# Hybrid decoder layer in float32: the first dilated group projected by token classes, its values re-sorted through DRAM

## Chip, cores and metric

One core of one Trainium2 chip runs the whole kernel. The metric is the device time of one execution in microseconds, as the median of several runs; lower is better.

## What is computed

Two layers, each on 512 tokens of width 1024, all in float32. A layer normalises `x`, multiplies it with one wide matrix `w_in`, and feeds three token mixers: a short gated convolution, a multi-head latent attention (MLA, 8 heads) and a dilated attention with 3 groups of 8 heads. The change touches the dilated attention alone:

```python
DIL_PATTERNS = ((128, 1), (512, 4), (2048, 16))       # (window, dilation) of the groups 0, 1, 2
dq = rmsnorm(dq.reshape(B, S, DIL_GROUPS, DIL_HEADS, DIL_HEAD_DIM), dil_q_norm_g[:, None, :])
dk = rmsnorm(dk.reshape(B, S, DIL_GROUPS, DIL_HEADS, DIL_HEAD_DIM), dil_k_norm_g[:, None, :])
dv = dv.reshape(B, S, DIL_GROUPS, DIL_HEADS, DIL_HEAD_DIM)
for gi, (window, dilation) in enumerate(DIL_PATTERNS):
    o_g, lse_g = dilated_group_attention(dq[:, :, gi], dk[:, :, gi], dv[:, :, gi], slopes[gi],
                                         dilation, window // dilation)
alpha = jax.nn.softmax(jnp.stack(lses, axis=0), axis=0)
o_c = jnp.sum(alpha[..., None] * jnp.stack(outs, axis=0), axis=0)
```

Group 0 attends to neighbouring tokens, so it works on four chunks of 128 consecutive tokens. Groups 1 and 2 attend to tokens 4 and 16 apart, so they work on four classes of 128 tokens, the tokens of one residue modulo 4.

## The kernel before

Products. TensorE multiplies float32 as three products of exact halves, `hi*hi + hi*lo + lo*hi`. `mm3` (L124) issues them, one line each: L126, L127 and L128. Weights are loaded into `wraw` by SyncE (L112), copied to the high half `whi` by ScalarE (L120) and reduced to the low half `wlo` by GpSimd or VectorE (L121); `wraw` has 5 buffers, and so have `whi` and `wlo`. The normalised input lies in `hhi` and `hlo`, 128 features by 512 tokens for each of 8 feature blocks.

Order of the tokens. The 512 columns of `hhi` and `hlo` are sorted by residue modulo 4: the columns of class r are 128 columns in a row (`of_class`, L175), and the tokens of a natural chunk c are every fourth column (`of_chunk`, L171).

The dilated projection. For each pair of heads p (0 to 3) and each group g (0 to 2), `dil_group` (L557) loads four weight tiles and runs `proj_n` (L147). This takes four token blocks, and in each 8 feature blocks by 3 products, so 96 matmuls for one p and g. The tokens are the stationary operand (128 columns of `hhi` or `hlo`, loaded anew for each matmul), and 384 columns of weights (q, k and v of two heads) move. Group 0 takes its tokens with `of_chunk`, groups 1 and 2 with `of_class`:

```python
yield from proj_n(wq, 384, of_class if g else of_chunk, evac)
```

After a token block, `evac` (L575) has ScalarE copy q and k to `nat` (L576) and the values to `vt` (L577). When the four blocks are done, VectorE and ScalarE find the norms (L584 to L587, L101 to L106), and GpSimd scales `nat` (L591). `dil_t` (L594) then transposes q and k: four TensorE transposes fill the four 128-column parts of one PSUM tile (L601), and ScalarE and VectorE copy the tile out (L611 to L620).

The attention of a pair. `dil_main` (L773) runs the scores (L646, L650, L656), their maxima and exponentials (L664, L667), a joint softmax over the groups whose sums go through DRAM twice (`dil_weights`, L672, with SyncE's L677, L679, L702 and L703), the scaling (L714, L718), more transposes (L734, L743) and the product with the values (`dil_pv`, L749, with the matmul on L765).

The order of the work. TensorE's order is written out by hand: `filler` (L887) is a list of projection steps, three matmuls in each, and the attention of MLA and of the dilated pairs is put between them at fixed numbers of steps. `dil_t` of a group stands 20 steps into the next projection (`T_LAG`). The other queues are ordered by a scheduler, and weight loads have a priority that lets them run ahead (L109). SyncE issues all DMAs in one queue, and one that waits holds up all behind it.

Of the kernel before, what the change touches and what calls it, by code (L numbers as in the profile page):

```python
# [28 lines left out]
C8, C2, W_RAW, W_BUF = 2, 38, 5, 5  # L29
# steps of projection between the steps of attention  # L30
F_LORA, F_P1, F_P2, F_MLA, F_TAIL, N_TAIL = 24, 6, 10, 1.2, 5.0, 28
# [9 lines left out]

# columns of the packed per-layer parameters
O_NORM, O_BG, O_CW, O_CB = 0, 8, 32, 44
# [4 lines left out]
def hybrid_kernel(ctx: ExitStack, tc: tile.TileContext, a: dict):  # L48
# [29 lines left out]

    # ---- constants
    ident = cp.tile([P, P], F32, name="ident")  # L80
# [14 lines left out]

    # ---- helpers
    def rsqrt(y, v, shape):
        """y = v ** -0.5 by Newton steps from the exponent-halving start."""
        sh = sp.tile(shape, I32, tag="rs_i", name=nm("rs_i"), bufs=3)
        t = sp.tile(shape, F32, tag="rs_t", name=nm("rs_t"), bufs=3)  # L100
        nc.vector.tensor_scalar(out=sh, in0=v.bitcast(I32), scalar1=1, scalar2=None, op0=ALU.logical_shift_right)  # L101
        nc.vector.tensor_scalar(out=y.bitcast(I32), in0=sh, scalar1=-1, scalar2=0x5F3759DF, op0=ALU.mult, op1=ALU.add)
        for _ in range(3):
            nc.vector.scalar_tensor_tensor(out=t, in0=y, scalar=-0.5, in1=v, op0=ALU.mult, op1=ALU.mult)
            nc.vector.tensor_tensor(out=t, in0=t, in1=y, op=ALU.mult)
            nc.vector.scalar_tensor_tensor(out=y, in0=t, scalar=1.5, in1=y, op0=ALU.add, op1=ALU.mult)  # L106
# [17 lines left out]
    def mm3(out, lhs, rhs, start, stop):  # L124
        """float32 product from exact halves: hi.hi + hi.lo + lo.hi"""
        nc.tensor.matmul(out, lhs[0], rhs[0], start=start, stop=False)  # L126
        nc.tensor.matmul(out, lhs[0], rhs[1], start=False, stop=False)  # L127
        nc.tensor.matmul(out, lhs[1], rhs[0], start=False, stop=stop)  # L128
# [6 lines left out]
    def proj_t(wsrc, box, X=None):  # L135
        """[128 features, 512 tokens] of h @ w for one 128-column tile of w_in; the PSUM tile goes to box;
        with X the unscaled input takes the place of h"""
        hi, lo = split_weights(1024, [(0, 1024, lambda t: t.rearrange("p (k n) -> p k n", k=KD), wsrc)])
        ps = psum("pj")
        for k in range(KD):  # L140
            cs = slice(k * P, (k + 1) * P)
            rhs = (X["hi"][k], X["lo"][k]) if X else (hhi[:, k], hlo[:, k])
            mm3(ps, (hi[:, cs], lo[:, cs]), rhs, k == 0, k == KD - 1)
            yield
        box.append(ps)

    def proj_n(wq, width, tok, evac):  # L147
        """[128 tokens, width] of h @ w per token block; wq: 4 split tiles of two k-chunks"""
        for c in range(NCH):
            ps = psum("pj")  # L150
            for k in range(KD):
                hi, lo = wq[k // 2]
                cs = slice((k % 2) * width, (k % 2 + 1) * width)
                mm3(ps[:, :width], (tok(hhi[:, k], c), tok(hlo[:, k], c)), (hi[:, cs], lo[:, cs]), k == 0, k == KD - 1)
                if k == KD - 1:
                    evac(c, ps)
                yield
# [10 lines left out]
    def tok_nat(c):  # L168
        return slice(c * P, (c + 1) * P)

    def of_chunk(t, c):  # L171
        """columns of the tokens of natural chunk c"""
        return t[:, c::NCH]

    def of_class(t, r):  # L175
        """columns of the tokens of residue r modulo 4"""
        return t[:, r * P:(r + 1) * P]
# [17 lines left out]
    def new_x(first=False):  # L195
        """x, x * gain in split form, and the running sum of squares"""
        return {"x": [], "hi": [], "lo": [], "acc": small([P, S], "acc", 1), "first": first}
# [15 lines left out]

    # products of a constant wake the tensor engine's clock while the first loads run
    wake = t2([P, P])
# [8 lines left out]
    for l in range(DEPTH):  # L224
        w_in = a["w_in"][l].rearrange("(k p) n -> p k n", p=P)
        last = l == DEPTH - 1

        # ---- low-rank inputs of the MLA branch from x * gain; the row scales follow
        lat = t8([P, NCH, W_LORA])
# [20 lines left out]
        def row_scale():  # L250
            """rows' rsqrt(mean(x ** 2) + eps)"""
            psv = psum("tr")
            for c in range(NCH):
                nc.tensor.matmul(psv[:, c:c + 1], of_chunk(X["acc"], c), ones, start=True, stop=True)
            v = small([P, NCH], "nv")
            r = small([P, NCH], "nr")
            nc.vector.tensor_scalar(out=v, in0=psv[:, :NCH], scalar1=1.0 / D, scalar2=EPS, op0=ALU.mult, op1=ALU.add)
            rsqrt(r, v, [P, NCH])
            return r
# [20 lines left out]

        # ---- h = rmsnorm(x), split
        psr = psum("tr")
# [13 lines left out]

        # derived parameters
        prm2 = small([P, 24 + 4], "prm2")
# [24 lines left out]
        def rope(dst, src, which, shape):  # L323
            """dst = rope(src * gain); shape [P, NCH, (heads,) 32]"""
            ta = rt[:, which, 0]
# [30 lines left out]
        def gate_y(y, which, f, zs):  # L356
            """y * silu(z), once both are there"""
            if (which, f) not in half_y:
                half_y[which, f] = zs
                return  # L360
            zs = half_y[which, f] if zs is None else zs
            nc.vector.scalar_tensor_tensor(out=y[f], in0=y[f], scalar=0.5, in1=zs, op0=ALU.mult, op1=ALU.mult)  # L362

        # ---- MLA
        ob = {}
# [4 lines left out]
        def mla_prep_w(p):  # L370
            """an even pair of heads brings the query weights of the next pair along"""
            o = 0 if p % 2 else 768
# [149 lines left out]
        def mla_main():  # L522
            """yields after each step on the tensor engine"""
            prep = iter(())
# [26 lines left out]

        # ---- dilated attention
        oc = {}
# [3 lines left out]
        def dil_group(p, g):  # L557
# [20 lines left out]

            yield from proj_n(wq, 384, of_class if g else of_chunk, evac)
            s2 = small([P, 16], "s16a")  # L580
# [13 lines left out]
        def dil_t(p, g):  # L594
# [3 lines left out]
            for i in range(2):  # L598
                ps = psum("tr")
                for c in range(NCH):  # L600
                    nc.tensor.transpose(ps[:, tok_nat(c)], nat[:, c, i * P:(i + 1) * P], ident)  # L601
                gg = prm2[:, 24 + g:25 + g] if i == 0 else prm[:, O_DK + g:O_DK + g + 1]
                if g == 0:
                    # per head: queries as high over low, keys as high over high, and the low keys of both heads
                    st = [t2([P, S], F32R) for _ in range(2)]
# [66 lines left out]
        def dil_weights(p):  # L672
            """maxima and sums of the strided groups to the natural order, joint weights, and back"""
            m = dil[p]
# [45 lines left out]
        def dil_trans(p, h):  # L720
            """transposed weights: g0 by key chunk, then g1, g2"""
            m = dil[p]
# [3 lines left out]
            for j2 in range(2):  # L726
# [10 lines left out]
                yield  # L737
            # the weights of g2 are zero outside the diagonal blocks of 32
            p2 = t2([P, S])
# [9 lines left out]
        def dil_pv(p):  # L749
            """the two heads fill the two halves of the array's columns"""  # L750
            m = dil[p]
# [21 lines left out]
        def dil_main(p):  # L773
            """yields the number of filler steps that follow"""
            for _ in dil_scores(p):
# [11 lines left out]
        def silu2(ps):  # L787
            """2 * silu(z) = z * (tanh(z / 2) + 1)"""
            th = t2([P, S])
            nc.scalar.activation(th, ps, AF.Tanh, scale=0.5)  # L790
            nc.vector.scalar_tensor_tensor(out=th, in0=th, scalar=1.0, in1=ps, op0=ALU.add, op1=ALU.mult)  # L791
            return th
# [9 lines left out]
        def conv_tile(f):  # L802
# [21 lines left out]
            for d in (1, 2):  # L824
                # the tokens d before, by the runs that the order of the columns leaves
                runs = [(cv[:, d * P:S], ac[:, 0:S - d * P])]
# [9 lines left out]

        # ---- gates, branch outputs, merge
        ys = {}
# [46 lines left out]

        # ---- schedule of the branches: projections fill the tensor engine while attention waits for other engines
        def filler():  # L887
# [53 lines left out]

        # ---- output projection and residual
        w_o = a["w_o"][l].rearrange("(k p) n -> p k n", p=P)
# [26 lines left out]
def _reorder(t):  # L970
    """tokens (first axis) by their residues modulo 4 and 16, the four chunks interleaved"""
    return t.reshape(4, 8, 4, 4, -1).transpose(3, 2, 1, 0, 4).reshape(t.shape)
# [6 lines left out]
def _constants():  # L979
# [6 lines left out]

    # tokens 128 h + 16 l + 4 j + r, in the order of (r, j, l, h)
    tok = _reorder(np.arange(S))
# [64 lines left out]
```

## Time and profile before

| what | value |
|---|---|
| median of 3 runs | 1546.23 us (1545.94 to 1547.9) |
| span of the profiled execution | 1547.1 us |
| TensorE matmuls busy | 1504.4 us, 97% |
| TensorE weight loads busy | 1327.6 us, 86% |
| VectorE, ScalarE, GpSimd busy | 799.7, 701.9 and 561.5 us |
| DMA | 132.14 MB, 85 GB/s over the span |

The profiled execution is known by its span alone; no time outside of it is listed. The span lies inside the range of the runs, 0.9 us above their median. PE is TensorE's row of matmuls, PEld its row of weight loads, which overlaps with PE; DVE is VectorE, ACT ScalarE, POOL GpSimd, and SPq the queue of SyncE. "L126" is line 126 of the kernel. The length of a matmul in the trace counts its way through the array as well, so the distance between the starts of two neighbours says what one costs.

### The profile page before, as it was taken

What the parts mean: (1) busy time and instruction counts of PE and PEld (TensorE: products, weight loads), DVE (VectorE), ACT (ScalarE), POOL (GpSimd) and SP (SyncE); (2) the same over time, 40 slices, a digit from 0 to 9 for tenths busy, and PEclk for the clock granted to TensorE, in tenths of its full rate; (3) what the DMA queues carried; (4) which work ended last, traced back from release to release, by engine and by line L of the source; (5) the groups of instructions that cost most, each with busy time, mean ns of one, the idle gap of its engine ahead of it and who ended that gap; (6) DMA issues with size and microseconds to landing.
All of it is one profiled execution on the core that took longest, in us unless ns stands there. A gap on an engine that the chain in (4) does not pass through costs nothing. (4 is left out here: it accounts for less than half of the span.)

```text
span 1547.1 us, 21464 instructions
## 1 busy us (share of the span) xinstructions
PE 1504.4 (97%) x7838; PEld 1327.6 (86%) x7838; DVE 799.7 (52%) x2120; ACT 701.9 (45%) x1600; POOL 561.5 (36%) x348
## 2 busy tenths in 40 slices
PE   8889999999999999999999899999999999999998
PEld 8777899999897878888898689999999888788887
DVE  7757675455555552221666767746463657411221
ACT  5445566637373533222344365646364545322220
POOL 5444243132224434444243433323122254344441
PEclk9999999999999999999999999999999999999999
DMA  8222113233243333333532311223132333233322
GB/s 234 58 82 55 42 51 82 56 83 80 59 111 89 83 82 95 96 104 103 179 97 72 86 35 42 54 70 98 47 92 62 98 97 96 82 95 96 109 82 82
DMA packets 230331, 132.14 MB, mean 85 GB/s; under 512 B 17745, under 2 KB 222929, under 8 KB 230225
## 3 DMA queue, kind: packets, MB, share of 16 engines
q1 hardware_dynamic: 230224, 130.77, 31.0%
q8 instruction: 62, 1.02, 0.3%
q14 instruction: 45, 0.36, 0.1%
HBM read 126.35 MB, written 4.39 MB: 85 GB/s over the span
## 5 line engine op out<-in xcount | busy, mean ns | idle before, releaser
L121 POOL TENSOR_TENSOR wlo<-wraw,whi 128x1024 fp32r<-128x1024 f32 (+1 forms) x184 | 426.3, 2319 | 665.5 <-ACT whi L120 643.5
L120 ACT CAST whi<-wraw 128x1024 fp32r<-128x1024 f32 (+4 forms) x249 | 235.6, 950 | 374.9 <-issue 191.4
L126 PE MATMUL pj<-hhi,whi 128*128 128x512 f32 x760 | 307.5, 405 | 0.6 <-DVE c L791 0.6
L127 PE MATMUL pj<-hlo,whi 128*128 128x512 f32 x760 | 298.7, 393 | 0.4 <-POOL hlo L290 0.4
L128 PE MATMUL pj<-hhi,wlo 128*128 128x512 f32 x760 | 299.0, 393 | 0.0
L126 PE MATMUL pj<-whi,hhi 128*128 128x384 f32 x768 | 293.7, 382 | 0.0
L127 PE MATMUL pj<-wlo,hhi 128*128 128x384 f32 x768 | 274.5, 357 | 0.0
L128 PE MATMUL pj<-whi,hlo 128*128 128x384 f32 x768 | 274.5, 357 | 0.0
L126 PEld LDWEIGHTS pj<-whi,hhi 128*128 128x128 f32 x768 | 179.8, 234 | 5.8 <-issue 2.1
L127 PEld LDWEIGHTS pj<-wlo,hhi 128*128 128x128 f32 x768 | 182.0, 237 | 0.8 <-DVE wlo L121 0.2
L128 PEld LDWEIGHTS pj<-whi,hlo 128*128 128x128 f32 x768 | 181.4, 236 | 0.0
L128 PEld LDWEIGHTS pj<-hhi,wlo 128*128 128x128 f32 x760 | 143.8, 189 | 31.2
L126 PEld LDWEIGHTS pj<-hhi,whi 128*128 128x128 f32 x760 | 144.4, 190 | 28.9 <-DVE c L791 1.4
L127 PEld LDWEIGHTS pj<-hlo,whi 128*128 128x128 f32 x760 | 144.3, 190 | 25.2 <-POOL hlo L290 0.8
L872 DVE SCALAR_TENSOR_TENSOR c<-c,sc 128x512 f32<-128x512 f32 x48 | 32.7, 685 | 239.8 <-PE sc L128 239.8
L121 DVE TENSOR_TENSOR wlo<-wraw,whi 128x768 fp32r<-128x768 f32 (+3 forms) x65 | 77.0, 1185 | 50.5 <-ACT whi L120 27.2
L667 ACT ACTIVATE c<-c,e 128x128 f32<-128x128 f32 (+1 forms) x192 | 79.9, 418 | 49.2 <-DVE e L664 49.2
L480 POOL TENSOR_SCALAR c<-c,mst 128x128 f32<-128x128 f32 (+1 forms) x64 | 35.7, 558 | 143.4 <-DVE mst L479 115.7
L591 POOL TENSOR_TENSOR c<-c,s16c 128x512 f32<-128x512 f32 x48 | 49.1, 1045 | 94.4 <-DVE s16c L106 94.4
L585 DVE TENSOR_REDUCE s16a<-c 128x8 f32<-128x512 f32 x48 | 32.7, 681 | 85.3 <-ACT c L584 85.1
L126 PE MATMUL sc<-c,whi 128*128 128x512 f32 x192 | 75.4, 393 | 0.0
L664 DVE CUSTOM_DVE_ANT_0 c<-sc,bias 128x128 f32<-128x128 f32 (+1 forms) x192 | 52.4, 319 | 44.2 <-PE sc L650 30.4
(201 smaller groups left out, 2435.5 us busy)
## 6 DMA issues: line engine op xcount, KB each, us to landing
wraw<-w_in SPq DMA_DIRECT2D x96, 512.0 KB, 3.9
wraw<-w_in SPq DMA_DIRECT2D x192, 192.0 KB, 2.8
wraw<-w_o SPq DMA_DIRECT2D x16, 512.0 KB, 4.3
bias<-bias SPq DMA_DIRECT2D x8, 512.0 KB, 3.6
wraw<-w_out_a SPq DMA_DIRECT2D x8, 512.0 KB, 3.4
wraw<-w_out_b SPq DMA_DIRECT2D x8, 512.0 KB, 3.4
wraw<-w_out_c SPq DMA_DIRECT2D x8, 512.0 KB, 3.4
wraw<-w_in SPq DMA_DIRECT2D x7, 416.0 KB, 3.5
```

The lines of the kernel that those rows point to most:

```text
L120: nc.scalar.copy(hi[:, c], raw[:, c])
L121: eng.tensor_sub(lo[:, c], raw[:, c], hi[:, c])
L126: nc.tensor.matmul(out, lhs[0], rhs[0], start=start, stop=False)
L127: nc.tensor.matmul(out, lhs[0], rhs[1], start=False, stop=False)
L128: nc.tensor.matmul(out, lhs[1], rhs[0], start=False, stop=stop)
L480: nc.gpsimd.tensor_scalar(out=pr[:, :n_], in0=pr[:, :n_], scalar1=st[:, 3:4], scalar2=1.0, op0=ALU.mult, op1=ALU.mult)
L585: nc.vector.reduce_sum(s2[:, 4 * c:4 * c + 8], sq[:, c:c + 2].rearrange("p c (h d) -> p (c h) d", d=64), axis=AX.X)
L591: eng.tensor_tensor(out=nv[:, i:i + 8], in0=nv[:, i:i + 8], in1=r2[:, i:i + 8].unsqueeze(2).to_broadcast([P, 8, 64]), op=ALU.mult)
L664: nc.vector.tensor_tensor_reduce(dst, src, b, op0=ALU.add, op1=ALU.min, scale=1.0, scalar=HIGHEST, accum_out=mc)
L667: nc.scalar.activation(dst, dst, AF.Exp, bias=mc, scale=-1.0, accum_out=sc_)
L872: nc.vector.scalar_tensor_tensor(out=ths[e], in0=ths[e], scalar=1.0, in1=ps, op0=ALU.add, op1=ALU.mult)
```

## The change

Group 0 projects classes of tokens as the other groups do, so its stationary operand is 128 columns in a row. What comes out is in the order of the classes, and two things bring it back to the order of the chunks. For q and k, each transpose writes to the PSUM tile with steps: the 128 columns of class c go to columns 32c to 32c + 31 of all four chunks. For the values, `vt` is written to a scratch in DRAM in one order and read back in the other.

```diff
-    def proj_n(wq, width, tok, evac):
+    def proj_n(wq, width, evac):
...
-                mm3(ps[:, :width], (tok(hhi[:, k], c), tok(hlo[:, k], c)), (hi[:, cs], lo[:, cs]), k == 0, k == KD - 1)
+                mm3(ps[:, :width], (of_class(hhi[:, k], c), of_class(hlo[:, k], c)), (hi[:, cs], lo[:, cs]), k == 0, k == KD - 1)
...
-            yield from proj_n(wq, 384, of_class if g else of_chunk, evac)
+            yield from proj_n(wq, 384, evac)
+            if g == 0:
+                vscr = dp.tile([S, P], F32, tag="vscr", name=nm("vscr"))
+                nc.sync.dma_start(vscr.rearrange("(r p) d -> p r d", p=P), vt)
+                nc.sync.dma_start(vt, vscr.rearrange("(p c) d -> p c d", p=P))
...
-                    nc.tensor.transpose(ps[:, tok_nat(c)], nat[:, c, i * P:(i + 1) * P], ident)
+                    dst = ps.rearrange("p (c x) -> p x c", c=NCH)[:, 32 * c:32 * c + 32] if g == 0 else ps[:, tok_nat(c)]
+                    nc.tensor.transpose(dst, nat[:, c, i * P:(i + 1) * P], ident)
```

The orders of TensorE, VectorE, ScalarE and GpSimd stay as they are, instruction by instruction; only SyncE's queue has new rows, 16 of them. In the new kernel all line numbers behind the change are 5 to 7 higher.

TensorE, the transposes of q and k of pair 1, group 0, in layer 0, before (`tr` is the PSUM tile, the third name is `nat`):

```order
L126 MATMUL pj_3140<-whi_3010,hhi 128x384
L127 MATMUL pj_3140<-wlo_3011,hhi 128x384
L128 MATMUL pj_3140<-whi_3010,hlo 128x384
L601 MATMUL tr_3153<-ident,c_599_2769 128x128 x4
L601 MATMUL tr_3164<-ident,c_599_2769 128x128 x4
L126 MATMUL pj_3140<-whi_3017,hhi 128x384
```

and the same place with the change:

```order
L126 MATMUL pj_3146<-whi_3016,hhi 128x384
L127 MATMUL pj_3146<-wlo_3017,hhi 128x384
L128 MATMUL pj_3146<-whi_3016,hlo 128x384
L608 MATMUL tr_3159<-ident,c_600_2772 128x32x4 x4
L608 MATMUL tr_3170<-ident,c_600_2772 128x32x4 x4
L126 MATMUL pj_3146<-whi_3023,hhi 128x384
```

Nothing moved there; the eight transposes write 32 runs of 4 scattered columns where they wrote 128 in a row.

SyncE's queue at the end of pair 1, group 0, before (`wraw` are weight loads, `bias` is the mask of the next pair, `scr` and `en` the first trip of the softmax sums through DRAM):

```order
L112 DMA wraw_3493<-w_in 128x3x128 x2
L112 DMA wraw_3500<-w_in 128x3x128 x2
L560 DMA bias_2739<-bias 128x2x512
L677 DMA scr_3178<-e_619_2901 128x4x8
L679 DMA en_3180<-scr_3178 128x32
L112 DMA wraw_3507<-w_in 128x3x128 x2
```

and with the change:

```order
L112 DMA wraw_3499<-w_in 128x3x128 x2
L112 DMA wraw_3506<-w_in 128x3x128 x2
L583 DMA vscr_2980<-c_601_2773 128x4x128
L584 DMA c_601_2773<-vscr_2980 128x512
L560 DMA bias_2742<-bias 128x2x512
L684 DMA scr_3184<-e_620_2904 128x4x8
L686 DMA en_3186<-scr_3184 128x32
L112 DMA wraw_3513<-w_in 128x3x128 x2
```

The two DMAs of the values stand ahead of the mask, of the softmax sums and of the next weights. It is the same for pairs 2 and 3.

SyncE's queue at the end of pair 0, group 0, before:

```order
L112 DMA wraw_2524<-w_in 128x3x128 x2
L112 DMA wraw_2741<-w_in 128x3x128 x2
L112 DMA wraw_2748<-w_in 128x3x128 x2
L112 DMA wraw_2755<-w_in 128x3x128 x2
L112 DMA wraw_2762<-w_in 128x3x128 x2
```

and with the change:

```order
L112 DMA wraw_2527<-w_in 128x3x128 x2
L112 DMA wraw_2744<-w_in 128x3x128 x2
L583 DMA vscr_2100<-c_368_1718 128x4x128
L584 DMA c_368_1718<-vscr_2100 128x512
L112 DMA wraw_2751<-w_in 128x3x128 x2
L112 DMA wraw_2758<-w_in 128x3x128 x2
```

Here only weight loads stand behind them, from the second tile of pair 1, group 0 on.

## Rows read from the trace of the kernel before

**Rows 1.** Part 1 of the page: busy us of each engine, share, instructions.

```profile
PE 1504.4 (97%) x7838; PEld 1327.6 (86%) x7838; DVE 799.7 (52%) x2120; ACT 701.9 (45%) x1600; POOL 561.5 (36%) x348
```

**Rows 2.** Waits of PE: who <- for whom, us in total, times, longest.

```profile
PE tr L455 <- DVE c L428: 10.5, 4, 4.1
PE tr L601 <- POOL c L591: 10.1, 11, 1.9
PE tr L491 <- DVE s24d L106: 3.8, 2, 1.9
```

**Rows 3.** Timeline of PE, pair 1, group 0: start us, us, instruction.

```profile
278.55 0.54 PE L126 MATMUL pj<-whi,hhi 128*128 128x384 f32 x1
278.93 0.41 PE L127 MATMUL pj<-wlo,hhi 128*128 128x384 f32 x1
...
281.48 0.39 PE L127 MATMUL pj<-wlo,hhi 128*128 128x384 f32 x1
...
285.92 0.39 PE L128 MATMUL pj<-whi,hlo 128*128 128x384 f32 x1
```

**Rows 4.** Timeline of PE, pair 1, group 1.

```profile
302.43 1.03 PE L601 MATMUL tr<-ident,c 128*128 128x128 f32 x8
303.22 0.42 PE L126 MATMUL pj<-whi,hhi 128*128 128x384 f32 x1
303.48 0.34 PE L127 MATMUL pj<-wlo,hhi 128*128 128x384 f32 x1
...
305.91 0.33 PE L126 MATMUL pj<-whi,hhi 128*128 128x384 f32 x1
```

**Rows 5.** Weight loads by line, 282 to 286 us (group 0): busy, mean ns.

```profile
L126 PEld LDWEIGHTS pj<-whi,hhi 128*128 128x128 f32 x7 | 2.3, 330 | 0.0
```

**Rows 6.** The same, 295.5 to 299 us (group 1).

```profile
L128 PEld LDWEIGHTS pj<-whi,hlo 128*128 128x128 f32 x5 | 0.9, 188 | 0.0
```

**Rows 7.** Timeline of PE, the MLA inputs, tokens by chunk, 416 columns.

```profile
11.00 0.40 PE L126 MATMUL pv<-whi,c 128*128 128x416 f32 x1
11.24 0.40 PE L127 MATMUL pv<-wlo,c 128*128 128x416 f32 x1
```

**Rows 8.** Timeline of PE, values: group 0 (PSUM in steps), then group 1.

```profile
337.99 1.73 PE L765 MATMUL pv<-c,c 128*64 128x256 f32 x16
...
341.32 1.09 PE L765 MATMUL pv<-c,c 128*64 128x128 f32 x16
```

**Rows 9.** Part 6 of the query on DMAs: KB each, median us to landing.

```profile
xr<-xnext SPq DMA_DIRECT2D x8, 256.0 KB, 2.8
xnext<-c SPq DMA_DIRECT2D x8, 256.0 KB, 2.0
```

**Rows 10.** Timeline of ACT, last copy of pair 1, group 0.

```profile
292.59 0.26 ACT L577 COPY c<-pj 128x128 f32<-128x128 f32 x1
```

**Rows 11.** Timeline of SPq, around the mask of the next pair.

```profile
301.10 0.37 SPq L560 DMA_DIRECT2D bias<-bias  x1
```

**Rows 12.** Timeline of SPq, a load behind pair 0, group 0.

```profile
218.39 0.90 SPq L112 DMA_DIRECT2D wraw<-w_in  x2
```

**Rows 13.** Timeline of ACT, the cast of those weights.

```profile
257.23 0.83 ACT L120 CAST whi<-wraw 128x768 fp32r<-128x768 f32 x1 [0.50 <-PE pj L128]
```

**Rows 14.** Timeline of POOL, scaling of pair 0, group 1.

```profile
249.05 2.05 POOL L591 TENSOR_TENSOR c<-c,s16c 128x512 f32<-128x512 f32 x2 [2.19 <-DVE s16c L106]
```

**Rows 15.** Timeline of PE, the transposes of pair 0, group 1.

```profile
252.34 1.03 PE L601 MATMUL tr<-ident,c 128*128 128x128 f32 x8
```

**Rows 16.** Windows: stretch and length, busy us (instructions), granted clock, DMA share, GB/s.

```profile
178.00:213.00 35.00, 35.00 (x188) 34.64 (x188) 23.81 (x71) 21.01 (x57) 11.21 (x14) 1.00 0.14 36
213.00:226.00 13.00, 13.00 (x88) 12.45 (x88) 10.64 (x33) 8.03 (x22) 6.00 (x7) 1.00 0.34 89
1231.90:1234.30 2.40, 2.40 (x10) 2.30 (x9) 2.37 (x11) 0.74 (x2) 0.00 (x0) 0.51 0.00 0
```

## The prediction

> **What bounds the kernel now.** I read the busy times first: TensorE's matmuls are busy 97% of the span, VectorE 52% and the others less, apart from TensorE's own weight loads at 86% [rows 1]. The list of its waits comes next: the longest entries are 10.5, 10.1 and 3.8 us [rows 2], small beside 1547. So time is what TensorE needs for its own list of instructions, and an edit counts by what it does to the pace of that list, or by a new wait on it.
>
> The pace is read from the timeline, from the start of one matmul to the start of the next. In group 0 of pair 1, 19 matmuls of 384 columns start between 281.48 and 285.92, one each 234 ns [rows 3]. In group 1 of the same pair, with the same shape, 14 start between 303.48 and 305.91, one each 174 ns [rows 4]. The reader should see that the difference is not in the moving columns. It is in the weight loads: one takes 330 ns where the tokens lie every fourth column [rows 5], and 188 ns where they lie in a row [rows 6]. A third place has stepped tokens too, the inputs of MLA: 416 columns move there, more than 384, and the distance is 0.24 us again [rows 7]. With stepped tokens the load sets the pace, whatever moves.
>
> **The change, part by part.**
>
> *The projection of group 0.* There are 4 pairs in 2 layers, and 96 matmuls in each, so 768. In TensorE's written order 104 of them come right behind an instruction of something else (27 in pair 0 of a layer, 7 in pair 1, 9 in pairs 2 and 3), and 664 behind another of the same projection. The 664 go from 234 to 174 ns each [rows 3, 4]: 664 x 0.060 = 39.8 us. The first one behind another instruction is slower in both groups: 278.55 to 278.93 is 0.38 us in group 0, 303.22 to 303.48 is 0.26 us in group 1 [rows 3, 4]. So 104 x 0.12 = 12.5 us. Together 52.3 us, all on the engine that sets the end.
>
> *The transposes of q and k.* 64 of them (8 in each group 0) now write to PSUM in steps of 128 elements. Eight of them take the 0.79 us from 302.43 to 303.22, 0.10 us each [rows 4]. No row has this step. The nearest one has steps of 4 elements: the product with the values writes so in group 0 (L761). Its 16 matmuls in the trace are, by the code, 12 of 256 columns and 4 of 128, and take 1.73 us. Group 1 writes in a row, and 16 of 128 columns take 1.09 us [rows 8]. Two heads run side by side, so these are 6 x 2 + 2 = 14 units of 128 columns against 8. The difference of 0.64 us for 6 units is 0.107 us a unit, and 8 units at that price and a tail of 0.2 us are the 1.09. A write with steps of 4 costs nothing there. I take nothing. The other end is that each new transpose takes twice its time, 64 x 0.10 = 6.4 us; below nothing is excluded, as the same columns pass.
>
> The Trainium skill (PSUM — Partial Sum Buffer, Specifications) says that PSUM has lines of 8 bytes and that any access pattern that is not contiguous slows matmuls significantly. That speaks against these writes, and by it the gain would be smaller by 6.4 us or more. The rows with steps of 4 elements, 16 bytes, do not agree with it, but no row has steps of 512 bytes.
>
> *The values through DRAM.* 8 writes and 8 reads of 256 KB. The rows have both kinds: 2.0 us to landing for a write of this size, 2.8 us for a read [rows 9]. With two issues of 0.4 us the trip takes some 5.5 us. In bytes it is 4.2 MB more on 132 MB, and the DMA engines are busy for 14 to 34% in these stretches [rows 16]. The price lies in SyncE's queue, which stands still during the trip. In pair 1 the last values are copied out at 292.85 [rows 10], so the trip ends at about 298.4. Next behind it is the mask, which goes out at 301.10 today, since it waits for the scores [rows 11]. 2.7 us remain. In pairs 2 and 3 the order is the same. In pair 0 weight loads stand behind: the first goes out at 218.39 [rows 12] and might go out 1 or 2 us later; its weights are not cast before 257.23, as the buffer behind it is not free [rows 13]. Nothing waits. The values themselves are used a whole pair later. I take nothing; the other end is under rival D.
>
> *What a faster group 0 brings forward.* Behind the end of each group 0 the work stands as now, since the orders of the four engines don't change. Inside it, a step of three matmuls shrinks from 0.70 to 0.52 us, and other engines have less time between steps. Pair 0 has the least room, with MLA beside it. VectorE is busy for 23.81 of 35 us there, and would be for 23.81 of some 28, 85%; in the 13 us behind it, it is at 10.64, 82%, while TensorE is busy throughout [rows 16]. So that load is borne today. The narrowest spot that I found is the transposes of pair 0, group 1: GpSimd is done at 251.10 [rows 14], TensorE needs it at 252.34 [rows 15], 1.2 us later. If VectorE comes out of the shorter stretch with a backlog of 2 us, about 1 us is lost here. I put 1 us for both layers, with bounds of 0 and the price of rival B.
>
> **The sum.** 52.3 - 0 - 0 - 1 = 51 us off the profiled execution's 1547.1, so 1496. The runs' median lies 0.9 us below that execution, so I forecast **1495.5 us** for the median. The gain is 3.3%.
>
> **The rivals.**
>
> *A. The forecast*, 1491 to 1503.
>
> *B. The other engines become late.* The faster group 0 takes away the room of VectorE, ScalarE and GpSimd, and TensorE waits for the preparation of MLA heads or for scaled q and k. For: such waits are there already [rows 2], and what waits is ordered by hand in steps, which get shorter. After TensorE had waited for its transposes near 1230 us the granted clock was 0.51 for 2.4 us, its lower level of 1.2 GHz [rows 16], which lost about half of these 2.4 us. Against: the 82% stretch runs without a wait, and pairs 1 to 3 have little beside group 0. Price: one more set like the existing entries of MLA (10.5 + 3.8 us for both layers [rows 2]), with 4 slow stretches at 1.2 us, is 19 us; half a set is 8. So 1503 to 1515.
>
> *C. The stepped writes to PSUM are slow*: 6.4 us at twice the time, 19 us at four times. So 1502 to 1515. For: the step is 32 times that of the nearest row. Against: that row shows no cost at all. The rule of the Trainium skill's page on PSUM, cited above, would give this rival.
>
> *D. SyncE's queue becomes the bound, and the kernel slower than before.* The two DMAs stand ahead of the mask and of the softmax sums of the pair before. A trip longer than 5.5 + 2.7 = 8.2 us holds the sums up, then the joint weights on VectorE, then the scaling of q and k of the next group behind them in that queue, and the transposes that TensorE has 20 steps into it wait for this today already (10.1 us in all [rows 2]). It decides in pairs 1 to 3, so 6 times. To end slower it has to lose 51 / 6 = 8.5 us each, a trip of over 17 us; at 20 us the time is 1496 + 6 x 11.8 = 1567. For: a queue in order, and a read that waits for the landing of the write. Against: the rows of such transfers, 2.0 and 2.8 us.
>
> *E. The pace of group 0 has another cause than the step of its tokens*, and the change brings nothing: 1546 to 1549. Against: the weight loads of MLA's inputs.
>
> **How the numbers follow.** A 0.72, B 0.13, C 0.08, D 0.02, E 0.03, and 0.02 for what I don't see. The range of 8 in 10 begins at 1490, a little under A's end for a term that I rounded down, and goes to 1510, which takes in A and about half of B and C. 0.2%, 3 us, is about what a measurement of this kernel can tell from no change. Faster by more than that are A, B, C: 0.94 with part of the unseen. No change 0.02, slower 0.04, D and parts of E and the unseen.
>
> **What would show it.** The weight loads of group 0 at 188 ns instead of 330, and its matmuls 174 ns apart. The eight groups shorter by 6 to 8 us each. The new transposes 0.10 us apart, or, for C, 0.2 and more. The write and the read of the values landing within 6 us of the last copy, and the mask's DMA still waiting for the scores; for D, the mask and the sums issued as soon as the read has gone out, and longer waits on the transposes in group 2. For B, new entries in the list of TensorE's waits in pair 0, and a granted clock under 1 behind them. The forecast is wrong if the time is over 1503: then the list of waits tells B from D, and the transposes tell C.

## The result, and the profile of the changed kernel

The changed kernel takes 1497.9 us (median of 4 runs, 1494.7 to 1499.6); the kernel before, run beside it, takes 1546.6 us. The ratio is 0.968, 95% interval [0.967, 0.970]: faster by 3.2%. On two later occasions the same kernel took 1501.9 and 1500.2 us, both 0.970 of the kernel before beside it. 1495.5 us was forecast, with a range of 1490 to 1510.

The changed lines moved the code down: what was L601 is L608 (the transposes of q and k), L591 is L596 (GpSimd's scaling). The values are written at L583 and read back at L584.

Busy time first, part 1 of the page of the changed kernel, against [rows 1]:

```profile
span 1495.3 us, 21490 instructions
PE 1451.1 (97%) x7838; PEld 1272.1 (85%) x7838; DVE 797.4 (53%) x2120; ACT 699.3 (47%) x1600; POOL 559.5 (37%) x348
```

TensorE has the same 7838 matmuls and is still busy for 97%. It is faster by being faster at its own list, not by waiting less. The timeline of TensorE in pair 1, group 0 of the changed kernel (start us, us, instruction) shows the pace:

```profile
265.07 0.34 PE L127 MATMUL pj<-wlo,hhi 128*128 128x384 f32 x1
...
267.33 0.33 PE L128 MATMUL pj<-whi,hlo 128*128 128x384 f32 x1
```

13 steps lie between these two starts, 2.26 us, so 174 ns each, as in [rows 4] and not the 234 ns of [rows 3]. The weight loads by line between 271 and 276 us, still group 0 (count, busy us, mean ns), read 188 ns where [rows 5] had 330:

```profile
L127 PEld LDWEIGHTS pj<-wlo,hhi 128*128 128x128 f32 x8 | 1.5, 188 | 0.0
```

From the first matmul of a group to the end of its last, in the first layer:

| group | before, us | changed, us | difference |
|---|---|---|---|
| pair 0, group 0 | 35.42 | 28.58 | -6.84 |
| pair 1, group 0 | 28.23 | 22.10 | -6.13 |
| pair 2, group 0 | 31.75 | 25.49 | -6.26 |
| pair 3, group 0 | 31.38 | 25.14 | -6.24 |
| pair 0, group 1 | 27.18 | 29.38 | +2.20 |
| pairs 1 to 3, group 1 | 20.29 each | 20.29 to 20.31 | 0 |

The second layer repeats this to 0.02 us. The four groups 0 give 25.5 us a layer, 50.9 in all; group 1 of pair 0 takes 4.4 us back. The groups 2 are left out here: those of pairs 2 and 3 change with the granted clock from one profile to the next, as a table below shows.

The waits of TensorE in the changed kernel (who <- for whom: us in total, times, longest) against [rows 2]:

```profile
PE tr L455 <- DVE c L428: 10.5, 4, 4.1
PE tr L608 <- POOL c L596: 9.7, 11, 1.9
...
PE tr L491 <- DVE s24d L106: 3.8, 2, 1.9
...
PE tr L491 <- DVE c L181: 1.7, 2, 0.8
...
PE tr L491 <- DVE rs_t L105: 0.6, 2, 0.3
PE tr L455 <- DVE c L460: 0.3, 2, 0.2
```

The three long entries are as before, or nearly so. The last three rows are new, small, and all in pair 0, group 1. TensorE's timeline shows where (in brackets: idle time before, and the releaser):

```profile
208.62 0.31 PE L491 MATMUL tr<-ident,c 128*128 128x128 f32 x1 [0.83 <-DVE c L181]
...
211.81 0.64 PE L455 MATMUL tr<-ident,c 128*96 128x128 f32 x4 [0.17 <-DVE c L460]
...
213.79 0.41 PE L491 MATMUL tr<-ident,c 128*128 128x128 f32 x2 [0.29 <-DVE rs_t L105]
```

Counted from start to start, these three places lose 1.0, 0.3 and 0.4 us against the kernel before, and a fourth transpose (L455 at 214.86) 0.3: 2.0 of the 2.2 us.

The transposes with stepped writes, TensorE's timeline in pair 1:

```profile
291.31 1.03 PE L608 MATMUL tr<-ident,c 128*128 128x128 f32 x8
292.10 0.42 PE L126 MATMUL pj<-whi,hhi 128*128 128x384 f32 x1
```

Eight of them in 0.79 us, as the eight with contiguous writes in [rows 4]. SyncE's queue behind pair 1, group 0:

```profile
282.35 0.43 SPq L583 DMA_DIRECT2D vscr<-c  x1
286.66 0.34 SPq L584 DMA_DIRECT2D c<-vscr  x1
289.98 0.37 SPq L560 DMA_DIRECT2D bias<-bias  x1
291.73 0.36 SPq L684 DMA_DIRECT2D scr<-e  x1
```

and the DMAs of the values (KB each, median us to landing):

```profile
vscr<-c SPq DMA_DIRECT2D x8, 256.0 KB, 4.3
c<-vscr SPq DMA_DIRECT2D x8, 256.0 KB, 2.6
```

The queue stands for the landing of the write, 4.3 us, and then sends the read and goes on. The mask at 289.98 has 3.0 us to spare behind it (289.98 - 286.66 - 0.34).

### The profile page after: what moved, and what is told of

Its sections match the earlier page's. It is cut to its first block, busy times and chain, and to the rows that moved or that the text cites. A ratio compares the mean times of both kernels' runs of the same rounds, so it can differ in the third digit from the quotient of the medians.

```text
span 1495.3 us, 21490 instructions
## 1 busy us (share of the span) xinstructions
PE 1451.1 (97%) x7838; PEld 1272.1 (85%) x7838; DVE 797.4 (53%) x2120; ACT 699.3 (47%) x1600; POOL 559.5 (37%) x348
## 5 line engine op out<-in xcount | busy, mean ns | idle before, releaser
L126 PE MATMUL pj<-whi,hhi 128*128 128x384 f32 x768 | 272.2, 354 | 0.0
L128 PE MATMUL pj<-whi,hlo 128*128 128x384 f32 x768 | 258.4, 336 | 0.0
L127 PE MATMUL pj<-wlo,hhi 128*128 128x384 f32 x768 | 257.6, 335 | 0.0
L126 PEld LDWEIGHTS pj<-whi,hhi 128*128 128x128 f32 x768 | 145.0, 189 | 5.7 <-issue 2.1
L127 PEld LDWEIGHTS pj<-wlo,hhi 128*128 128x128 f32 x768 | 145.2, 189 | 0.6
L128 PEld LDWEIGHTS pj<-whi,hlo 128*128 128x128 f32 x768 | 144.4, 188 | 0.0
L121 DVE TENSOR_TENSOR wlo<-wraw,whi 128x768 fp32r<-128x768 f32 (+3 forms) x65 | 77.8, 1197 | 42.4 <-ACT whi L120 25.5
L596 POOL TENSOR_TENSOR c<-c,s16c 128x512 f32<-128x512 f32 x48 | 49.1, 1043 | 91.3 <-DVE s16c L106 91.3
L126 PE MATMUL sc<-c,whi 128*128 128x512 f32 x192 | 75.5, 393 | 0.0
L128 PE MATMUL sc<-c,wlo 128*128 128x512 f32 x192 | 74.9, 390 | 0.0
L127 PE MATMUL sc<-c,whi 128*128 128x512 f32 x192 | 74.8, 390 | 0.0
```

The costliest lines, as they stand in the source:

```text
L121: eng.tensor_sub(lo[:, c], raw[:, c], hi[:, c])
L596: eng.tensor_tensor(out=nv[:, i:i + 8], in0=nv[:, i:i + 8], in1=r2[:, i:i + 8].unsqueeze(2).to_broadcast([P, 8, 64]), op=ALU.mult)
```

## The experiments

**The two halves of the change apart.** One kernel keeps the projection by classes and leaves out the re-sorting; the other keeps the old projection and does the re-sorting on top of it. A third is the changed kernel again.

```diff
 e1: projection alone
-            if g == 0:
-                vscr = ...
-                nc.sync.dma_start(... vt)
-                nc.sync.dma_start(vt, ...)
-                    dst = ps.rearrange(...) if g == 0 else ps[:, tok_nat(c)]
+                    dst = ps[:, tok_nat(c)]
 e2: re-sorting alone
-            yield from proj_n(wq, 384, evac)
+            yield from proj_n(wq, 384, of_class if g else of_chunk, evac)
```

> The changed kernel once more, beside the others on the same chip: 1494 to 1500 us.

> The change without what brings the order back: group 0 projects classes, the transposes write in a row and the values don't go through DRAM, so group 0 works on tokens of the wrong order. Theory (the step of the stationary tokens is all of the gain, the re-sorting costs nothing): the time of the changed kernel, 1495 to 1500 us, 47 to 51 us under the kernel before. Rival 1 (the stepped PSUM writes or the trip through DRAM cost something): 3 to 10 us under the changed kernel. Rival 2 (the gain comes from something else, such as the moved queue): clearly over 1500.

> The re-sorting alone: group 0 projects chunks as before, and its q, k and values are sorted once more on top, so they end in a wrong order; the orders of the engines are those of the changed kernel. Theory: nothing, 1546 to 1549 us. Rival 1 (stepped PSUM writes cost): 64 transposes at twice their time give +7 us, 1553. Rival 2 (SyncE's queue holds up the softmax sums): +5 us or more.

Measured: changed kernel again 1501.9 us (ratio 0.970, [0.968, 0.972]), a little above what was expected; projection alone 1497.9 (0.968, [0.967, 0.970]); re-sorting alone 1546.5 (1.000, [0.999, 1.001]). So the whole gain is the projection, and on the kernel before the re-sorting, transposes and DRAM trips together, costs nothing within 0.1%.

On top of the new projection the two medians of this round stand 4.0 us apart (1501.9 and 1497.9), which is where rival 1 put them. The runs overlap (1497.3 to 1503.5 and 1497.7 to 1501.1), and the profiles show another cause for most of it. All other groups of the two agree to 0.2 us; the four groups 2 of pairs 2 and 3 don't. In them TensorE waits for GpSimd before the transposes of group 1, and behind that wait the granted clock falls in some profiles and not in others. Where it falls, its mean over the group is 0.92 to 0.93, and 1.00 where it does not:

| profile | four groups 2 of pairs 2 and 3, together, us | of the four, with the lower clock |
|---|---|---|
| before | 91.0 | 3 |
| changed | 87.3 | 1 |
| e0, changed again | 92.3 | 4 |
| e1, projection alone | 88.5 | 2 |
| e2, re-sorting alone | 87.0 | 1 |
| e10 (below) | 89.0 | 2 |
| e11, changed again (below) | 91.0 | 3 |

The changed kernel itself has it once, three times and four times, so e0 and e1 give no price for the re-sorting. The kernel with the projection alone shows the same new wait, which so has nothing to do with the re-sorting:

```profile
PE tr L491 <- DVE c L181: 1.7, 2, 0.8
```

**A trip twice as long.**

```diff
 e3, behind the read of the values
+                vscr2 = dp.tile([S, P], F32, tag="vscr2", name=nm("vscr2"))
+                nc.sync.dma_start(vscr2.rearrange("(p c) d -> p c d", p=P), vt)
+                nc.sync.dma_start(vt, vscr2.rearrange("(p c) d -> p c d", p=P))
```

> The changed kernel with a second trip of the values through DRAM (same order in and out, so the results stay). In the trace of the changed kernel the queue is free 3.0 us before the mask of the next pair goes out in pair 1. A second trip takes the landing of the first read, 2.6 us, a write of 2 to 4.3 us and two issues, 5.3 to 7.6 us together. Theory (the queue has a margin of about 3 us, and what exceeds it comes out at the transposes of group 1, six times): 1 to 4 us late each, 6 to 20 us in all, 1504 to 1518. Rival (nothing waits for this queue, there is room everywhere): within 2 us of the changed kernel.

Measured: 1502.4 us (0.971, [0.970, 0.972]), 0.5 us from the changed kernel beside it (1501.9). The expected loss did not come. SyncE's queue of this kernel in pair 1:

```profile
283.21 0.43 SPq L583 DMA_DIRECT2D vscr<-c  x1
287.61 0.34 SPq L584 DMA_DIRECT2D c<-vscr  x1
290.33 0.33 SPq L586 DMA_DIRECT2D vscr<-c  x1
292.63 0.32 SPq L587 DMA_DIRECT2D c<-vscr  x1
293.05 0.39 SPq L560 DMA_DIRECT2D bias<-bias  x1
293.53 0.42 SPq L687 DMA_DIRECT2D scr<-e  x1
```

The softmax sums leave at 293.53 in place of 291.73, of which 0.86 us is a later start of the whole trip: they are about 1 us later. The two writes carry the same values: the first, in rows of 512 bytes, holds the queue for 4.4 us (283.21 to 287.61), the second, in rows of 2 KB, for 2.3 (290.33 to 292.63). The DMA engines were busier beside the first (0.59 against 0.31 of their time), so the length of the rows need not be all of it. TensorE's waits changed places (its transposes are L611 here):

```profile
PE pj L127 <- DVE wlo L121: 7.7, 4, 2.1
...
PE tr L611 <- POOL c L599: 3.2, 5, 1.3
```

6.5 us less on the transposes, 7.7 us more on low halves of weights. VectorE's order also came out a little different in the later pairs, so this is no clean price of a delay. It shows only that a second trip in the queue did not make the kernel slower.

**What the pace of group 0 hangs on.** The tokens of group 0 are taken with steps of 4, 2, 3 and 1 elements in the four pairs.

```diff
-            yield from proj_n(wq, 384, evac)
+            yield from proj_n(wq, 384, of_class if g else step_of[p], evac)
```

> Group 0 of the four pairs takes its stationary tokens with step 4 (pair 0), 2 (pair 1), 3 (pair 2) and 1 (pair 3), in both layers; the re-sorting is left out, so the groups 0 hold other tokens than the reference's and the attention of the dilated branch is of the wrong tokens. The kernel before showed 330 ns a load and 234 ns from matmul to matmul at step 4, the changed kernel 188 ns and 174 ns at step 1. Theory: the Trainium skill, page SBUF - State Buffer, section on cachelines, states lines of 16 bytes of which at least two reads in a row must fall into one for full speed; by it step 2 (8 bytes, two tokens to a line) runs as step 1, 188 and 174 ns, step 4 (one to a line) as before, 330 and 234 ns, and step 3 (12 bytes, now one, now two to a line) as step 4 or between. Rival: any step other than 1 loads at 330 ns, then steps 2 and 3 show 330 and 234 ns as well. Second rival: the load grows with the bytes between tokens, then step 2 shows about 235 ns and step 3 about 280 ns. Time, from the measured 51 us for all eight groups 0 (6.4 us each): by the theory two to four of the eight are slow, so 13 to 26 us over the changed kernel's 1498 us, 1511 to 1524; by the first rival six, 1536; by the second between.

Measured: 1513.9 us (one run). The weight loads by line, in a stretch of group 0 of pairs 0, 1, 2 and 3 (steps 4, 2, 3, 1):

```profile
L128 PEld LDWEIGHTS pj<-whi,hlo 128*128 128x128 f32 x14 | 4.6, 330 | 0.0
...
L128 PEld LDWEIGHTS pj<-whi,hlo 128*128 128x128 f32 x11 | 2.1, 195 | 0.0
...
L128 PEld LDWEIGHTS pj<-whi,hlo 128*128 128x128 f32 x17 | 4.3, 253 | 0.0
...
L128 PEld LDWEIGHTS pj<-whi,hlo 128*128 128x128 f32 x8 | 1.5, 188 | 0.0
```

Step 2 is nearly as good as step 1 (195 ns a load, most of them 194, against 188; group 0 of pair 1 takes 22.12 us against 22.10), step 3 costs 253 ns, step 4 330. Both rivals fall: not every step is slow, and the cost does not grow evenly. Counted in pieces of 16 bytes, 128 tokens touch 128 pieces at step 4, 96 at step 3, 64 at step 2 and 32 at step 1; 330 / 128 and 253 / 96 are both 2.6 ns. So these loads fit about 2.6 ns for each 16-byte piece, but not under 188 ns. That is an estimate from four points of one run, and another count might fit them too. It agrees with the Trainium skill (SBUF — State Buffer, Specifications): lines of 16 bytes, two hits a line for full bandwidth. Here step 2, with two tokens to a piece, is at 194 ns, and step 4, with one, at 330.

The length of a load in the trace is more than what it adds to the pace: at step 4 330 ns go with 234 from start to start. At step 3 the matmuls come 178 ns apart (median), though a load takes 253: group 0 of pair 2 is only 0.9 us longer than at step 1 (26.36 against 25.49). How loads and matmuls overlap, these runs don't show. And pair 0, back at step 4, has a group 0 of 35.41 us and a group 1 of 27.20, as before the change: the 2.2 us are lost because group 0 of pair 0 is faster, whatever the other pairs do.

**Two attempts at the waits that move steps of the schedule.**

```diff
 e5: T_LAG, steps before the transposes
-                        for _ in range(T_LAG):
+                        for _ in range(T_LAG + 6 if prev[1] == 1 and p else T_LAG):
 e6: steps of projection for each step of MLA
-            due += F_TAIL if tail else F_MLA
+            due += F_TAIL if tail else 1.5 if at[0] == (0, 0) else F_MLA
```

> The changed kernel with the transposes of group 1 six filler steps later in pairs 1 to 3 (26 steps instead of 20 into group 2). In the changed kernel they wait there for GpSimd's second scaling, 0.7 to 2.4 us in each of six places, 9.7 us in all. Theory: six steps of 0.55 us are 3.3 us, more than the longest of these waits, and nothing else moves, so the six waits go, and with them the stretches at the lower clock level behind the longer ones: 8 to 12 us less than the changed kernel, 1486 to 1490 us. Rival: GpSimd's scaling is late because something before it is late on every engine, and TensorE only waits elsewhere, as it did with two DRAM trips; then 1496 to 1500 us, with a new entry of 5 us or more among TensorE's waits.

> The changed kernel with 1.5 filler steps for each step of the MLA branch in place of 1.2, while the projection of pair 0 group 0 runs and there alone. It tests where the term of the prediction for what a faster group 0 brings forward was too small: group 1 of pair 0 was longer by 2.2 us in each layer, with new waits of its transposes for VectorE's splits. Theory: the MLA steps followed each other faster since the filler steps between them are shorter, and left VectorE a backlog for group 1; with 1.5 the steps come as far apart as before, the waits of L491 for VectorE's L181 and L105 (1.7 and 0.6 us) go, and group 1 of pair 0 takes 27 us again: 3 to 4.5 us less, 1493.5 to 1495 us. Rival: the backlog comes from the casts and low halves of the weights of the next tiles; then group 1 of pair 0 stays at 29 us and the time at 1497 to 1499 us.

> The changes of the two runs before it together. If each gains what its theory says, they add up, since they lie in different places (pair 0 group 1; pairs 1 to 3 group 2): 1482 to 1487 us, against 1498 us of the changed kernel. If only the later transposes gain, 1486 to 1490; if neither does, 1496 to 1500.

Measured: later transposes 1507.1 us (0.974, [0.972, 0.975]), MLA spread 1523.7 (0.984, [0.983, 0.986]), both 1530.8 (0.989, [0.987, 0.991]). All are slower than the changed kernel, by 9, 26 and 33 us against its 1497.9 (by 5, 22 and 29 against the 1501.9 of e0); the theories of all three fell. With later transposes, the longest row of TensorE's waits is this:

```profile
PE tr L608 <- DVE c L743: 18.2, 6, 5.2
```

VectorE's timeline of this kernel, before the longest of these waits ends:

```profile
443.82 5.99 DVE L725 TENSOR_SCALAR c<-c,w12p 128x128 f32<-128x128 f32 x15
...
450.43 0.69 DVE L743 COPY c<-tr 128x512 f32<-128x512 f32 x1
```

The wait for GpSimd went, as expected. But six steps on, the transposes stand behind those of the attention weights (L741), which write to the same ring of PSUM tiles. Its tiles come free by VectorE's copies (L743), and those stand behind 6 us of scaling (L725). The old place, with its wait of 1 to 2 us, was the cheaper one. With MLA spread, group 1 of pair 0 grew to 37.1 us, and new waits came up in several places:

```profile
PE pj L126 <- ACT c L577: 8.4, 2, 4.2
...
PE tr L608 <- DVE c L181: 4.6, 4, 1.8
```

The steps of MLA that left group 0 have to be done later; where exactly each new wait begins I have not followed up.

**The backlog on VectorE, without touching TensorE's order.** VectorE is busy for 9.08 of the 9.50 us from 206 to 215.5 us in the changed kernel:

```profile
206.00:215.50 9.50, 8.08 (x49) 6.64 (x48) 9.08 (x25) 6.14 (x15) 4.16 (x4) 1.00 0.60 168
```

(The columns are those of [rows 16]; the engines are PE, PEld, DVE, ACT, POOL, in this order.) That alone does not tell the two kernels apart. In the kernel before, VectorE is busy for 8.41 of 9.00 us at the same place, and TensorE never stops:

```profile
213.00:222.00 9.00, 9.00 (x61) 8.53 (x61) 8.41 (x26) 5.95 (x17) 3.25 (x4) 1.00 0.48 127
```

VectorE's timeline of the changed kernel there:

```profile
206.55 1.53 DVE L121 TENSOR_TENSOR wlo<-wraw,whi 128x768 fp32r<-128x768 f32 x1
...
208.08 0.40 DVE L181 TENSOR_TENSOR c<-tr,c 128x256 fp32r<-128x256 f32 x1
...
211.68 1.77 DVE L104 SCALAR_TENSOR_TENSOR rs_t<-s16c,s16b 128x16 f32<-128x16 f32 x1
...
213.97 0.17 DVE L104 SCALAR_TENSOR_TENSOR rs_t<-s16c,s16b 128x16 f32<-128x16 f32 x1
```

and GpSimd's beside it:

```profile
205.43 1.84 POOL L121 TENSOR_TENSOR wlo<-wraw,whi 128x768 fp32r<-128x768 f32 x1 [0.25 <-ACT whi L120]
...
211.58 1.83 POOL L121 TENSOR_TENSOR wlo<-wraw,whi 128x768 fp32r<-128x768 f32 x1 [0.50 <-DMA wraw<-w_in]
```

The same instruction (L104, 16 columns) takes 1.77 us beside GpSimd's and 0.17 us two microseconds later; the long one ends at 213.45, 0.04 us behind GpSimd's (213.41). The low half at 206.55 takes 1.53 us, and GpSimd is at its own until 207.27. The same instructions in the kernel before, GpSimd's timeline:

```profile
209.66 1.84 POOL L121 TENSOR_TENSOR wlo<-wraw,whi 128x768 fp32r<-128x768 f32 x1 [0.25 <-ACT whi L120]
...
216.53 1.84 POOL L121 TENSOR_TENSOR wlo<-wraw,whi 128x768 fp32r<-128x768 f32 x1 [0.49 <-DMA wraw<-w_in]
```

and VectorE's:

```profile
211.91 0.96 DVE L121 TENSOR_TENSOR wlo<-wraw,whi 128x768 fp32r<-128x768 f32 x1 [0.80 <-ACT whi L120]
...
212.86 0.40 DVE L181 TENSOR_TENSOR c<-tr,c 128x256 fp32r<-128x256 f32 x1
...
216.84 1.55 DVE L104 SCALAR_TENSOR_TENSOR rs_t<-s16c,s16b 128x16 f32<-128x16 f32 x1
```

GpSimd's had ended, at 211.50, when VectorE's low half began, and that took 0.96 us. So the shorter group 0 has pushed two instructions on top of each other that used to follow one another. L104 met GpSimd's instruction before the change as well (1.55 us), so it lengthened the stretch in both kernels.

How much each of this counts is read from L181 at 208.08, which the first of the late transposes needs. In the kernel before, L181 ended at 213.26, and the transpose came 1.5 us later:

```profile
214.77 0.27 PE L491 MATMUL tr<-ident,c 128*128 128x128 f32 x1
```

With the change, TensorE begins group 1 7.15 us earlier (206.14 for 213.29), but VectorE the low half only 5.36 us earlier (206.55 for 211.91) and L181 only 4.78 (208.08 for 212.86). So VectorE came out of the shorter group 0 some 1.8 us late, and its meeting with GpSimd added 0.6; together they use up the 1.5 us and make the wait of 0.83. Two edits try to relieve VectorE, each on one tile of weights:

```diff
-                     w_dil[:, 2 * q + k, :, c0:c0 + P]) for k in range(2)], pool=q in G_POOL))
 e8
+                     ... pool=q in ((0, 2, 3) if (p, g) == (0, 1) else G_POOL)))
 e9
+                     ... pool=q in ((2,) if (p, g) == (0, 2) else G_POOL)))
 e10
+                     ... pool=q in ((0, 2, 3) if (p, g) == (0, 1) else (2,) if (p, g) == (0, 2) else G_POOL)))
```

> The changed kernel with one more low half of weights on GpSimd in place of VectorE: the fourth tile of pair 0 group 1. TensorE's order is the same, VectorE's is shorter by one instruction a layer. In the changed kernel that instruction runs at 206.55 for 1.53 us, in the kernel before its like took 0.96; beside it GpSimd is at the third tile (205.43, 1.84 us). Theory: group 1 of pair 0 is longer by 2.2 us a layer since VectorE is full there (9.08 of 9.50 us busy) and everything that TensorE waits for stands behind this instruction; without it the waits for L181 and L460 (0.83 and 0.17 us a layer) go, group 1 of pair 0 takes 27.5 to 28.5 us in place of 29.2, and the time is 1.5 to 3.5 us less than the changed kernel's 1498: 1494.5 to 1496.5. Rival: GpSimd, with two halves in a row (1.84 us each), is late with the scaling of MLA's weights (208.25 now) by about 0.9 us and TensorE waits for that; group 1 stays at 29 us or more. In either case the time alone may not tell, the length of group 1 does.

> The changed kernel with one low half fewer on GpSimd: the first tile of pair 0 group 2 goes to VectorE. In the changed kernel GpSimd makes it at 211.58 for 1.83 us, and beside it VectorE's L104 on 16 columns takes 1.77 us, where its next ones take 0.17. Theory: while GpSimd runs such an instruction VectorE cannot start another of this kind (the Trainium skill, page Trainium Architecture - The Big Picture, section What this means for kernel authors, states an exclusive lock between the two); without GpSimd's instruction L104 takes 0.2 us, VectorE pays 0.95 us for the half itself, gains 0.6 us, and the wait for L105 (0.29 us a layer) goes or halves; group 1 of pair 0 takes 28.5 to 29, the time is 0 to 1.5 us less than the changed kernel's 1498. Rival: L104 is long for another cause, such as waiting for an operand; then it stays at 1.5 us or more, VectorE has 0.95 us more to do, and group 1 of pair 0 takes 30 us or more.

> The edits of the two runs before it together: the fourth tile of pair 0 group 1 to GpSimd, the first tile of group 2 to VectorE. Each alone took 0.5 to 0.9 us off group 1 of pair 0 in each layer (28.7 and 28.5 us in place of 29.2 to 29.4) and removed its own wait, for L181 or for L105. Theory: these are separate pieces of the same backlog and add up, so group 1 takes 27.8 to 28.1 us and the kernel 2 to 3 us less than the changed kernel run beside it. Rival: the one takes away what the other gained, since GpSimd's second half runs on into the time where VectorE now makes its own; then group 1 stays at 28.5 and the gain at 1 to 1.5 us.

> The changed kernel itself, beside the run before it on the same chip, as the measure for it: 1496 to 1502 us, group 1 of pair 0 29.2 to 29.4 us.

Measured, with the length of pair 0, group 1 (first and second layer):

| kernel | time, us | ratio to before, interval | pair 0, group 1, us |
|---|---|---|---|
| e8 | 1498.9 | 0.969 [0.967, 0.970] | 28.71, 28.74 |
| e9 | 1499.2 | 0.969 [0.968, 0.971] | 28.54, 28.53 |
| e10, both | 1496.4 | 0.967 [0.966, 0.969] | 27.84, 27.86 |
| e11, changed kernel beside e10 | 1500.2 | 0.970 [0.968, 0.972] | 29.41, 29.41 |

In e8 the 0.83 us wait for L181 is gone, but not the one for L460, and group 1 stays above the 27.5 to 28.5 us that were expected; in e9 that for L105 is gone, and L104 in VectorE's timeline takes

```profile
212.35 0.16 DVE L104 SCALAR_TENSOR_TENSOR rs_t<-s16c,s16b 128x16 f32<-128x16 f32 x1
212.43 0.94 DVE L121 TENSOR_TENSOR wlo<-wraw,whi 128x768 fp32r<-128x768 f32 x1
```

0.16 us, with GpSimd's instruction away. That is the plain test of the meeting; e8 takes a whole instruction off VectorE and does not tell one from the other. Together the two edits take 1.55 us off each layer's group 1, 3.1 us, and the medians stand 3.8 us apart. Three of the five runs of e10 (1493.1 to 1497.2) lie below all four of e11 (1496.9 to 1500.9). In TensorE's timeline one wait is left there:

```profile
212.11 0.64 PE L455 MATMUL tr<-ident,c 128*96 128x128 f32 x4 [0.24 <-DVE c L460]
```

This version is faster than the kernel before, and by the length of group 1 faster than the changed kernel by 3.1 us; the times alone do not part the last two, as their intervals overlap. The two single edits were expected to save 1.5 to 3.5 and 0 to 1.5 us; their medians do not show it. The length of group 1 does: against e11 it is 1.4 us (e8) and 1.75 us (e9) for both layers.

## Why the prediction was right

The forecast (rival A) held, 2.4 us under the median, and its steps can be checked one by one. That it came so near is in part luck: two terms were off, both to the fast side, and in the profiled executions the granted clock gave back 3.7 us, as the last point says.

- *The projection of group 0*: predicted 52.3 us, measured 50.9 by the eight group lengths, and shown to be the whole gain by the kernel that does nothing else (e1). The loads at 188 ns and the pace of 174 ns came out as read from group 1.
- *The transposes*: nothing predicted, nothing found (0.79 us for eight; re-sorting alone at ratio 1.000). Rival C is out. By the rule of the Trainium skill (PSUM — Partial Sum Buffer, Specifications) these writes should have been slower; this trace does not agree with it, at steps of 512 bytes.
- *The values through DRAM*: nothing predicted, nothing found, but two sizes inside were wrong and made up for each other. The write takes 4.3 us to landing and not 2.0. The row that I took as the nearest, of the same 256 KB, writes rows of 2 KB, while this one writes rows of 512 bytes; the two writes of e3 point the same way. And the queue does not stand for the read, so the mask had 3.0 us to spare, near the 2.7 predicted. Rival D is out: even a second trip did not make the kernel slower.
- *What a faster group 0 brings forward*: this term was mis-sized, 1 us predicted, 4.4 measured. The place was wrong as well: the transposes that I called the narrowest spot kept their 1.2 us (GpSimd done at 246.11, TensorE there at 247.35). The loss is at the start of group 1, in transposes of MLA that wait for VectorE. I had argued that VectorE's 82% there were borne before. What that left out is that a shorter group 0 leaves VectorE less time before these transposes: it comes out some 1.8 us late, near the backlog of 2 us that the prediction names as a case, but meets a place with 1.5 us to spare that the prediction did not look at. The change also moves GpSimd's instructions against VectorE's: the low half that took 0.96 us then took 1.53. Moving two tiles between the two engines gave back 3.1 of the 4.4 us, of which the meeting that the change made is a part; the other edit removed one that was there before. It is rival B's mechanism at the price of a quarter of the set that I had costed for it.
- *The rest*: 50.9 - 4.4 is 46.5 us, and the medians differ by 48.7. What is left, some 2 us, is within the spread of the runs (1494.7 to 1499.6 of one kernel). The two profiled executions differ by 51.8 us, and 3.7 of the 5.3 us over 46.5 lie in the groups 2 of pairs 2 and 3, which had the lower granted clock three times before and once after. As this comes and goes with one kernel, it is not shown to be an effect of the change; on the two later occasions the medians differ by 45.1 and 46.3 us.

## What to carry to other kernels

Where loads of the stationary operand set TensorE's pace, look at how many 16-byte pieces one load touches, and store the operand so that there are at least two wanted elements to a piece; re-sorting the results behind cost nothing here that these runs can tell from noise, since it fell on engines and queues with room. When a stretch of the bound engine gets shorter, don't only compare busy shares of the others: look which of their instructions now run at the same time, VectorE's and GpSimd's above all. A step moved to avoid a wait has to be followed on every ring that it shares. And before a difference of a few microseconds is explained, look at whether the granted clock fell at the same places in both profiles.

## What the hardware showed unexpectedly

- A load of 128 x 128 elements of 4 bytes took 188 ns at step 1, 195 at step 2, 253 at step 3 and 330 at step 4 (e4).
- Transposes that write to PSUM in steps of 512 bytes took 0.10 us each, as contiguous ones.
- VectorE's L104 on 16 columns took 1.77 us beside an instruction of GpSimd and 0.16 us once that was moved away; a low half of weights took 1.53 against 0.95 us. The Trainium skill (Trainium Architecture — The Big Picture, What this means for kernel authors) states an exclusive lock on the port pair that the two engines share. The trace agrees: L104 ended with GpSimd's instruction, at 213.45 and 213.41.
- A write of 256 KB to DRAM landed after 4.3 us in rows of 512 bytes, 2.0 us in rows of 2 KB [rows 9]; the traffic beside them was not held equal.
- After the same wait the granted clock falls in one run and not in another. From 377 to 381 us the first profile of the changed kernel has (columns as in [rows 16])

```profile
377.00:381.00 4.00, 4.00 (x28) 3.93 (x27) 3.75 (x15) 1.81 (x4) 0.00 (x0) 1.00 0.00 0
```

and the profile of its repetition e0 has

```profile
377.00:381.00 4.00, 3.60 (x14) 3.60 (x15) 3.57 (x15) 1.38 (x2) 0.35 (x1) 0.57 0.00 0
```

2.4 GHz throughout in the first, mostly 1.2 GHz (0.57) in the second, with half the matmuls done; group 2 of pair 2 was 1.5 us longer there. The waits ahead of it were the same, 1.3 and 0.6 us in both. What decides it stays open.
